# Down projection of a decoder layer: low parts of u in half tiles, adding transfers later, and one more pair by seven products

## The chip, the cores and the metric

The kernel runs on one core of one Trainium2 chip. The metric is the time of one execution on the device in microseconds (us), lower is better. The kernel before has a median of 1049.46 us over 3 runs (1048.84 to 1049.66).

## The reference, cut to what matters

One decoder layer on 256 positions of width 2048, in float32: a normed input projection, two attentions of 8 heads each, an output projection with a residual, and then an MLP with hidden width 8192. The change lies in the MLP:

```python
h = _rmsnorm(x, norm_mlp_pre[layer])
u = jnp.square(jax.nn.relu(h @ w_up[layer]))          # 256 x 8192
x = x + _rmsnorm(u @ w_down[layer], norm_mlp_post[layer])   # 8192 -> 2048
```

## The kernel before, in words

**Three matmuls for one product.** Every float32 operand is split into a high part (`hi`, ScalarE, line 306) and the remainder (`lo`, VectorE, line 307). A product is then hi·hi + lo·hi + hi·lo, that is three matmuls of 128x128 by 128x512. Weights come as `raw` tiles of 128x1024 (512 KB) on SyncE's queue and are split before use; a `Weights` object emits loads and splits up to six tiles ahead of TensorE.

**The down projection.** It runs in two halves of 1024 output columns (c = 0, 1), each over 64 blocks of 128 rows of u, which are taken as 32 pairs, numbered 0 to 31. A plain pair takes 2 x 4 products (24 matmuls). A pair in `DOWN_SEVEN[c]` is done by seven products of sums, after Strassen (21 matmuls). In the first half these are pairs 5, 7, 9, 11, then 15, 17, 19, 21, then 25, 27, 29; in the second every odd pair from 3 to 27. For such a pair p, GpSimd's queue fetches both weight blocks in one transfer of 1 MB (line 374, into `ab_down`, or by turns into `c` in the first half and `u01` in the second). VectorE makes the sums t and u of the weights (lines 361, 365, 366, destination `st_down`) and, for the u side, `four_sums` (lines 992 to 994) and their split into `s`. The sums of pair p are placed on VectorE ahead of the two `raw` splits of the plain pair p-1. In the first half the split `s` of a pair that both halves share is written to DRAM (`keep_s`); the second half reads it back (line 404) and needs neither `four_sums` nor the split.

**Where u's low part comes from.** u is produced in 16 tiles of four blocks (two pairs) each. While the up projection runs, `lo_away` writes -hi of a tile to DRAM (ScalarE, lines 960 and 962) and later adds u to it there (GpSimd's queue with an accumulating transfer, line 967), which leaves u - hi = lo in `ukeep`. In the down projection `split_u` makes `uhi` again on ScalarE and reads the whole low tile (512 KB) back into one of two `ulo` buffers on GpSimd's queue (line 979). Tile 0 is the exception: both times it is split on VectorE.

**What sets the order.** Each engine and each queue works in the order in which the program emits. GpSimd's queue is one such order: a transfer that waits there holds up all behind it. `Flow` is a clock by which chains such as `lo_away` are placed between matmuls; a `yield 16.0` puts the next step at least 16 us of that clock later.

**Between the halves.** The first half's four accumulators y are joined with the parts in `c` (line 1193), squared on ScalarE (line 1145) and multiplied by the gain (line 1197) in `half_evac`, while the second half begins.

Of the kernel before, what the change touches and what calls it, by code (L numbers as in the profile page):

```python
# [18 lines left out]
F32 = mybir.dt.float32  # L19
# [7 lines left out]
P = 128  # L27
# [236 lines left out]
def layer(nc, tc, io):  # L264
# [38 lines left out]
    def split(hi, lo, src, g=None):  # L303
        if g is not None:
            return split_gain(hi, lo, src, g)
        nc.scalar.activation(hi, src, AF.Copy)  # L306
        nc.vector.tensor_tensor(out=lo, in0=src, in1=hi.bitcast(F32), op=OP.subtract)  # L307
# [6 lines left out]
    def tok(t, k, b):  # L314
        return t[:, k, b * P:(b + 1) * P]
# [617 lines left out]
    def up_evac(j, b, i, acc, order):  # L933

        yield UP_STEP * order
        r = late["up"].tile([P, 512], F32, tag="r", bufs=2, name=f"r{j}_{b}")
        nc.scalar.activation(r, acc, AF.Relu, scale=rstd2[b])
# [12 lines left out]
        if b and j:  # L950
            flow.start(lo_away(j), 2.0 + 4.0 * (j % 2))

    def lo_away(g):

        ukeep[g] = dram.tile([P, CW], F32, name=f"ukeep{g}")
        u = uT[g].rearrange("p k s -> p (k s)")
        for h in range(2):
            c = slice(h * 512, (h + 1) * 512)
            t = late["up"].tile([P, 512], F32, tag="r", bufs=2, name=f"neg{g}_{h}")
            nc.scalar.activation(t.bitcast(F32R), u[:, c], AF.Copy, scale=-1.0)  # L960
            yield 1.0
            nc.scalar.dma_start(out=ukeep[g][:, c], in_=t)
            yield 7.0
        yield 16.0
        for h in range(2):
            c = slice(h * 512, (h + 1) * 512)
            nc.gpsimd.dma_start(out=ukeep[g][:, c], in_=u[:, c], accum_op=OP.add)
            yield 2.0

    def split_u(c, g):  # L970
        if (c, g) == (0, 0):
            uh, ul = [wp.tile([P, CW], F32R, tag=w, bufs=W_BUFS, name=f"u{w}0").rearrange("p (k s) -> p k s", k=4)
                      for w in ("hi", "lo")]
        else:
            uh, ul = [dpl["dp"].tile([P, 4, S], F32R, tag=f"u{w}", bufs=2, name=f"u{w}{c}_{g}") for w in ("hi", "lo")]
        u, h, l = [x.rearrange("p k s -> p (k s)") for x in (uT[g], uh, ul)]
        if g:
            nc.scalar.activation(h, u, AF.Copy)
            nc.gpsimd.dma_start(out=l.bitcast(F32), in_=ukeep[g])
# [153 lines left out]
    ssd = [con.tile([P, 4], F32, name=f"ssd{b}") for b in range(NB)]  # L1133

    def down_mm(c, u, k, b, n, w, first, last):
        three(y[b][2 * c + n], [tok(u[x], k % 4, b) for x in range(2)], [t[:, 0, n * 512:n * 512 + 512] for t in w],
              first, last)

    def spare(i, n):
# [3 lines left out]
    def square(n, b):  # L1143
        junk = dpl["dp"].tile([P, 512], BF16, tag="junk", bufs=1, name=f"junkd{n}{b}")
        nc.scalar.activation(junk, y[b][n], AF.Square, accum_out=ssd[b][:, n:n + 1])
# [41 lines left out]

    def half_evac(more, g_half):

        for n in range(2):  # L1190
            for b in range(NB):
                tt, out = nc.vector.tensor_tensor, more[b, n]
                tt(out=y[b][n], in0=y[b][n], in1=out, op=OP.add)
                yield 1.0
                square(n, b)
                yg[n, b] = out
                tt(out=out, in0=y[b][n], in1=g_half[n], op=OP.mult)
# [14 lines left out]
    for c in range(2):  # L1212

        for i, (b, n) in enumerate(PARTS):
            y[b][2 * c + n] = bank(4 * c + i, f"y{b}{2 * c + n}")
        accs = {(b, n): y[b][2 * c + n] for b, n in PARTS}
        ws = DOWN_SEVEN[c]
        for t, (what, k, tiles) in enumerate(wide_d[c]):
            g = (2 * k if what == "w" else k) // 4
            u = us[c, g]  # L1220
            if g >= GT - 2 and c:
                break
            if what == "k":
                w = weights.get(tiles[0])
                for b, n in PARTS:
                    down_mm(c, u, k, b, n, w, t == 0, t == len(wide_d[c]) - 1)
                    flow.pump()
                weights.free(tiles[0])
            else:
                if k == ws[0]:  # L1230
                    if not c:
                        flow.finish(*u_last)
                    else:
                        flow.finish(h_evac)
                    m = {i: bank(4 * (1 - c) + o, f"md{i}_{c}") for o, i in enumerate((1, 6, 7, 5))}
                blocks = [[tok(u[x], 2 * (k % 2) + kk, bb) for x in range(2)] for kk, bb in ((0, 0), (1, 0), (1, 1))]
                seven_products(tiles, (blocks, left.pop((c, k))), accs, m, k == ws[0], k == ws[-1])
                if k == ws[-1]:
                    more = close([spare(10, i) for i in range(4)] if c else closing(), m)
                if not c and k in SHARED:  # L1240
                    keep_s(k)
            nxt = (c, g + 1) if g < GT - 1 else (1, 0)
            if nxt not in us:
                us[nxt] = split_u(*nxt)
            if (c, what, k) == (0, "k", 3):
                weights.limit += 1
            if (c, what, k) == (0, "k", 36):
                g_half = [late["up"].tile([P, 512], F32, tag="r", bufs=2, name=f"g_half{n}") for n in range(2)]
                for n in range(2):
                    load_gain(n, g_half[n])  # L1250
            if (c, what, k) == (1, "k", 40):
                flow.start(x_back())
                for n in (2, 3):
                    load_gain(n, spare(4, n))
        if not c:
            h_evac = flow.start(half_evac(more, g_half))

    tail = {k: tiles[0] for what, k, tiles in wide_d[1] if k >= 4 * (GT - 2) and what == "k"}
    for g in (GT - 2, GT - 1):
        for b, n in PARTS:  # L1260
            for kk in range(4):
                k = 4 * g + kk
                w = weights.get(tail[k])
                if g < GT - 1:
                    down_mm(1, us[1, g], k, b, n, w, False, kk == 3)
                else:
                    three_more(y[b][2 + n], [tok(us[1, g][x], kk, b) for x in range(2)],
                               [t[:, 0, n * 512:n * 512 + 512] for t in w])
# [52 lines left out]
```

## Time and profile before

| what | value |
|---|---|
| median of 3 runs | 1049.46 us |
| the profiled execution | 1049.74 us |
| its span, first to last instruction | 1047.9 us |
| around the span | 1.8 us |
| granted TensorE clock, mean | 0.998 |
| TensorE busy | 1035.3 us (99%) |
| VectorE busy | 834.0 us (80%) |
| ScalarE busy | 644.5 us (62%) |
| DMA, mean over the span | 237 GB/s |

Times in the traces count from the span's start. The first half of the down projection runs from about 703 to 871.6 us, the second to about 1039 us; the up projection lies ahead of it from about 363 us on. A row of a timeline gives the start, the duration, the engine, the source line, the operation and its tiles (output, then inputs), how many instructions were merged, and in brackets how long the engine had been idle and what released it. For a DMA the duration is that of issuing it; "to landing" is from issue until its data has arrived.

### The profile page before, as it was taken

To read this page: it belongs to the slowest core of one execution; us is meant where nothing else is said; L and a number is where in the kernel's file an instruction comes from. 1 tells how busy PE (TensorE), PEld (TensorE's weight loads), DVE (VectorE), ACT (ScalarE), POOL (GpSimd) and SP (SyncE) were. 2 spreads that over 40 slices of the span, in tenths; PEclk is the share of its full clock that TensorE was granted. 3 is DMA by queue.
4 is the path that set the end of the run, shared out by engine and by line. 5 is a ranking of instruction groups with operands and counts; after the bars stand their busy time and mean duration, and the time that the engine had idled before them with its cause. 6 is when DMAs were issued, how large, how long until landed. Compare 5 with 4: busy or idle time off the path is not lost.

```text
span 1047.9 us, 13455 instructions
## 1 busy us (share of the span) xinstructions
PE 1035.3 (99%) x4828; PEld 860.3 (82%) x4828; DVE 834.0 (80%) x1122; ACT 644.5 (62%) x884; POOL 90.4 (9%) x134
## 2 busy tenths in 40 slices
PE   9999999999999999999999999999999999999996
PEld 6888889888888788888888888788888888788785
DVE  6676536567557669999999999796989888998895
ACT  6674436565555566675766767666757564866661
POOL 0000000000000000111101011011201001212100
PEclk9999999999999999999999999999999999999999
DMA  9975447454447295758879587589997977789862
GB/s 301 368 230 150 139 131 240 142 162 156 145 164 235 84 370 180 252 177 263 238 237 289 174 251 232 164 289 346 306 380 250 362 260 236 276 314 338 330 233 81
DMA packets 89395, 248.21 MB, mean 237 GB/s; under 512 B 7920, under 2 KB 12528, under 8 KB 88944
## 3 DMA queue, kind: packets, MB, share of 16 engines
q1 hardware_dynamic: 61984, 162.03, 45.9%
q0 software_dynamic: 22592, 77.08, 23.3%
q10 hardware_dynamic: 4752, 8.24, 2.2%
q8 instruction: 38, 0.62, 0.2%
q14 instruction: 29, 0.24, 0.1%
HBM read 222.16 MB, written 25.17 MB: 236 GB/s over the span
## 4 chain that ended last, share of the span: by engine, by line
PE 86%; DVE 6%; DMA 3%; issue 2%; ACT 2%; SPq 0%; POOL 0%; DVEq 0%; POOLq 0%; ACTq 0%
PE acc_u L296 21%; PE y L296 20%; PE acc_o L296 8%; PE m L296 6%; PE md L296 5%; PE acc_v L296 4%; PE acc_qk L296 4%; DVE lo L307 3%; PE acc_ckv L296 2%; PE acc_ukv L296 2%; PE acc_q L296 2%; PE acc_cq L296 2%; PE acc_k L296 2%; PE acc_uq L296 2%; PE rt L300 1%
## 5 line engine op out<-in xcount | busy, mean ns | idle before, releaser
L307 DVE TENSOR_TENSOR lo<-raw,hi 128x1024 fp32r<-128x1024 f32 (+3 forms) x207 | 233.5, 1149 | 81.8 <-ACT hi L306 81.1
L306 ACT ACTIVATE hi<-raw 128x1024 fp32r<-128x1024 f32 (+3 forms) x207 | 203.3, 996 | 67.4 <-DMA raw<-in_w_in 15.4
L296 PE MATMUL acc_u<-hi,hT_hi 128*128 128x512 f32 x356 | 141.7, 398 | 0.0
L296 PE MATMUL acc_u<-hi,hT_lo 128*128 128x512 f32 x356 | 139.2, 391 | 0.4 <-DVE hT_lo L307 0.4
L296 PE MATMUL acc_u<-lo,hT_hi 128*128 128x512 f32 x356 | 138.8, 390 | 0.0
L296 PE MATMUL y<-hi,ulo 128*128 128x512 f32 x352 | 137.1, 390 | 0.8 <-DMA ulo<-ukeep 0.8
L296 PE MATMUL y<-lo,uhi 128*128 128x512 f32 x352 | 137.1, 390 | 0.7 <-DVE lo L307 0.7
L296 PE MATMUL y<-hi,uhi 128*128 128x512 f32 x352 | 137.3, 390 | 0.0
L310 ACT ACTIVATE hi<-raw,gcol 128x1024 fp32r<-128x1024 f32 x74 | 83.0, 1147 | 31.9 <-DMA raw<-in_w_up 20.1
L311 DVE SCALAR_TENSOR_TENSOR lo<-raw,gcol,hi 128x1024 fp32r<-128x1024 f32 x74 | 92.4, 1278 | 11.1 <-ACT hi L310 11.0
L296 PEld LDWEIGHTS acc_u<-hi,hT_lo 128*128 128x128 f32 x356 | 66.8, 188 | 14.9 <-DVE hT_lo L307 0.8
L296 PEld LDWEIGHTS y<-hi,ulo 128*128 128x128 f32 x352 | 66.0, 188 | 15.0 <-DMA ulo<-ukeep 1.2
L296 PEld LDWEIGHTS y<-lo,uhi 128*128 128x128 f32 x352 | 66.1, 188 | 14.6 <-DVE lo L307 1.2
L296 PEld LDWEIGHTS acc_u<-lo,hT_hi 128*128 128x128 f32 x356 | 67.0, 188 | 13.0
L296 PEld LDWEIGHTS acc_u<-hi,hT_hi 128*128 128x128 f32 x356 | 66.9, 188 | 12.8
L296 PEld LDWEIGHTS y<-hi,uhi 128*128 128x128 f32 x352 | 66.1, 188 | 13.7
L306 ACT ACTIVATE hi<-u 128x1024 fp32r<-128x1024 f32 (+1 forms) x38 | 37.5, 990 | 47.6 <-DVE u L366 34.7
L307 DVE TENSOR_TENSOR lo<-st_down,hi 128x1024 fp32r<-128x1024 f32 x48 | 57.5, 1219 | 1.1 <-ACT hi L306 1.0
L296 PE MATMUL md<-hi,s 128*128 128x512 f32 x144 | 52.1, 389 | 0.0
L306 ACT ACTIVATE hi<-st_down 128x1024 fp32r<-128x1024 f32 x48 | 49.8, 1050 | 3.4 <-DVE st_down L366 2.9
L296 PE MATMUL acc_o<-hi,mixT_hi 128*128 128x512 f32 x128 | 51.8, 405 | 0.0
L296 PE MATMUL acc_o<-hi,mixT_lo 128*128 128x512 f32 x128 | 50.2, 392 | 0.0
(330 smaller groups left out, 2171.1 us busy)
## 6 DMA issues: line engine op xcount, KB each, us to landing
raw<-in_w_down SPq DMA_DIRECT2D x80, 512.0 KB, 6.1
raw<-in_w_up SPq DMA_DIRECT2D x76, 512.0 KB, 6.4
raw<-in_w_in SPq DMA_DIRECT2D x55, 512.0 KB, 5.1
ab<-in_w_up POOLq DMA_DIRECT2D x22, 1024.0 KB, 6.1
raw<-in_w_out SPq DMA_DIRECT2D x32, 512.0 KB, 4.4
ulo<-ukeep POOLq DMA_DIRECT2D x30, 512.0 KB, 6.7
ab_down<-in_w_down POOLq DMA_DIRECT2D x13, 1024.0 KB, 9.2
ukeep<-neg ACTq DMA_DIRECT2D x30, 256.0 KB, 4.4
```

The source lines that it names most:

```text
L296: nc.tensor.matmul(out, a, b, start=start, stop=stop)
L300: nc.tensor.transpose(out, a, ident)
L306: nc.scalar.activation(hi, src, AF.Copy)
L307: nc.vector.tensor_tensor(out=lo, in0=src, in1=hi.bitcast(F32), op=OP.subtract)
L310: nc.scalar.activation(hi, src, AF.Copy, scale=g)
L311: nc.vector.scalar_tensor_tensor(out=lo, in0=src, scalar=g, in1=hi.bitcast(F32), op0=OP.mult, op1=OP.subtract)
```

## The change

It does five things.

1. In the first half 12 pairs are done by seven products in place of 11: 5 to 15 and 19 to 29 by twos.
2. u's low tile is read back as two half tiles of 256 KB, one for each pair, into four buffers. `load_lo` numbers them by pair (0 to 31 in the first half, 32 to 63 in the second) and after the step of pair k emits the load for pair k+3.
3. Tile 0 goes through DRAM like the others, so that the second half reads its low part too and VectorE splits it once.
4. The adding transfers of `lo_away` come 34 us of the program's clock later in place of 16.
5. In `half_evac` the product by the gain of one accumulator comes behind the addition of the next.

How the instructions move on GpSimd's queue at the start of the down projection. The number behind `ulo0_` is the tile of two pairs, the number behind `ulo` in the new kernel is the pair; `ukeep` from `ab` are adding transfers of tiles 12 and 13; `ab_down` and `c` from `in_w_down` are the fetches for pairs 5, 7 and 9 in this order. Before:

```order
L979 DMA ulo0_1_6408<-ukeep1_3831 128x1024
L967 DMA ukeep12_6087<-ab_3502 128x512
L374 DMA ab_down_6373<-in_w_down 128x2x1024
L967 DMA ukeep12_6087<-ab_3502 128x512
L967 DMA ukeep13_6161<-ab_3502 128x512 x2
L979 DMA ulo0_2_6529<-ukeep2_4169 128x1024
L374 DMA c_3504<-in_w_down 128x2x1024
L979 DMA ulo0_3_6616<-ukeep3_4236 128x1024
L374 DMA ab_down_6373<-in_w_down 128x2x1024
```

And in the changed kernel:

```order
L989 DMA ulo2_6416<-ukeep1_3835 128x512
L989 DMA ulo3_6418<-ukeep1_3835 128x512
L374 DMA ab_down_6382<-in_w_down 128x2x1024
L989 DMA ulo4_6485<-ukeep2_4174 128x512
L989 DMA ulo5_6537<-ukeep2_4174 128x512
L989 DMA ulo6_6580<-ukeep3_4241 128x512
L967 DMA ukeep12_6093<-ab_3502 128x512
L374 DMA c_3504<-in_w_down 128x2x1024
L967 DMA ukeep12_6093<-ab_3502 128x512
L989 DMA ulo7_6628<-ukeep3_4241 128x512
L967 DMA ukeep13_6166<-ab_3502 128x512 x2
L989 DMA ulo8_6704<-ukeep4_4559 128x512
```

Before, the fetch for pair 7 (`c`) stands behind two low tiles, whose buffers are both empty. Now it stands behind `ulo6`, the fifth half tile, which needs the buffer of `ulo2` and so the end of pair 2. The next row behind the last shown is the fetch for pair 9, now behind `ulo8` and so behind the end of pair 4; before it stood behind `ulo0_3`, which needs the buffer of tile 1 and so the end of pair 3.

GpSimd's queue in the second half, around the fetch for pair 21 (the `u01` row). `s1_19` is the split that was kept for pair 19. Before:

```order
L374 DMA ab_down_6373<-in_w_down 128x2x1024
L404 DMA s1_19_8501<-skeep19_7299 128x1024
L979 DMA ulo1_9_8522<-ukeep9_5391 128x1024
L374 DMA u01_3505<-in_w_down 128x2x1024
L404 DMA s1_21_8584<-skeep21_7396 128x1024
```

In the changed kernel (half tile 52 belongs to pair 20 of the second half and needs the buffer of pair 16):

```order
L374 DMA ab_down_6382<-in_w_down 128x2x1024
L404 DMA s1_19_8573<-skeep19_7334 128x1024
L989 DMA ulo51_8593<-ukeep9_5396 128x512
L989 DMA ulo52_8652<-ukeep10_5712 128x512
L374 DMA u01_3505<-in_w_down 128x2x1024
L404 DMA s1_21_8658<-skeep21_7425 128x1024
```

Before, the fetch follows `s1_19`, which needs the end of pair 15. Now `ulo52` stands ahead of it, and the fetch follows the end of pair 16. The low part of pair 20, which stood behind the fetch and `s1_21` before, now stands ahead of both.

VectorE at the beginning of the second half. `y` are the first half's accumulators, `c` the parts joined to them. Before:

```order
L307 TENSOR_TENSOR lo_7825<-ab_down,hi_7824 128x512
L1193 TENSOR_TENSOR y_6374<-y_6374,c 128x512
L1197 TENSOR_TENSOR c<-y_6374,g_half_7240 128x512
L307 TENSOR_TENSOR lo_7849<-ab_down,hi_7848 128x1024
L1193 TENSOR_TENSOR y_6376<-y_6376,c 128x512
L1197 TENSOR_TENSOR c<-y_6376,g_half_7240 128x512
L307 TENSOR_TENSOR lo_7869<-st_down,hi_7868 128x1024
```

Changed:

```order
L307 TENSOR_TENSOR lo_7881<-ab_down,hi_7880 128x512
L1208 TENSOR_TENSOR y_6383<-y_6383,c 128x512
L1208 TENSOR_TENSOR y_6385<-y_6385,c 128x512
L307 TENSOR_TENSOR lo_7907<-ab_down,hi_7906 128x1024
L1203 TENSOR_TENSOR c<-y_6383,g_half_7269 128x512
L1208 TENSOR_TENSOR y_6384<-y_6384,c 128x512
L307 TENSOR_TENSOR lo_7927<-st_down,hi_7926 128x1024
```

The product by the gain (now line 1203) no longer stands right behind the addition to the same accumulator; another addition and a split lie between.

The diff:

```diff
-DOWN_SEVEN = ((5, 7, 9, 11, 15, 17, 19, 21, 25, 27, 29), range(3, 28, 2))
+DOWN_SEVEN = ((5, 7, 9, 11, 13, 15, 19, 21, 23, 25, 27, 29), range(3, 28, 2))
...
-        if b and j:
+        if b:
             flow.start(lo_away(j), 2.0 + 4.0 * (j % 2))
...
             nc.scalar.dma_start(out=ukeep[g][:, c], in_=t)
             yield 7.0
-        yield 16.0
+        yield 34.0
         for h in range(2):
...
     def split_u(c, g):
         if (c, g) == (0, 0):
-            uh, ul = [wp.tile([P, CW], F32R, tag=w, bufs=W_BUFS, name=f"u{w}0").rearrange("p (k s) -> p k s", k=4)
-                      for w in ("hi", "lo")]
-        else:
-            uh, ul = [dpl["dp"].tile([P, 4, S], F32R, tag=f"u{w}", bufs=2, name=f"u{w}{c}_{g}") for w in ("hi", "lo")]
-        u, h, l = [x.rearrange("p k s -> p (k s)") for x in (uT[g], uh, ul)]
-        if g:
-            nc.scalar.activation(h, u, AF.Copy)
-            nc.gpsimd.dma_start(out=l.bitcast(F32), in_=ukeep[g])
-        else:
-            split(h, l, u)
-        return uh, ul
+            uh, ul = [wp.tile([P, CW], F32R, tag=w, bufs=W_BUFS, name=f"u{w}0") for w in ("hi", "lo")]
+            split(uh, ul, uT[0].rearrange("p k s -> p (k s)"))
+            uh, ul = [x.rearrange("p (k s) -> p k s", k=4) for x in (uh, ul)]
+            return uh, [ul[:, 0:2], ul[:, 2:4]]
+        uh = dpl["dp"].tile([P, 4, S], F32R, tag="uhi", bufs=2, name=f"uhi{c}_{g}")
+        nc.scalar.activation(uh.rearrange("p k s -> p (k s)"), uT[g].rearrange("p k s -> p (k s)"), AF.Copy)
+        load_lo(2 * (c * GT + g) + 1)
+        return uh, [u_lo.pop(2 * (c * GT + g) + h) for h in range(2)]
+
+    u_lo = {}
+    next_lo = [2]
+
+    def load_lo(upto):
+
+        for i in range(next_lo[0], min(upto + 1, 4 * GT)):
+            g, h = i // 2 % GT, i % 2
+            t = u_lo[i] = dpl["dp"].tile([P, 2, S], F32R, tag="ulo", bufs=4, name=f"ulo{i}")
+            nc.gpsimd.dma_start(out=t.rearrange("p k s -> p (k s)").bitcast(F32), in_=ukeep[g][:, h * 512:(h + 1) * 512])
+            next_lo[0] = i + 1
...
     def half_evac(more, g_half):
 
+        def half_gain(b, n):
+            yg[n, b] = more[b, n]
+            nc.vector.tensor_tensor(out=more[b, n], in0=y[b][n], in1=g_half[n], op=OP.mult)
+
+        done = []
         for n in range(2):
             for b in range(NB):
-                tt, out = nc.vector.tensor_tensor, more[b, n]
-                tt(out=y[b][n], in0=y[b][n], in1=out, op=OP.add)
+                nc.vector.tensor_tensor(out=y[b][n], in0=y[b][n], in1=more[b, n], op=OP.add)
+                square(n, b)
                 yield 1.0
-                square(n, b)
-                yg[n, b] = out
-                tt(out=out, in0=y[b][n], in1=g_half[n], op=OP.mult)
-                yield 1.0
+                if done:
+                    half_gain(*done.pop())
+                    yield 1.0
+                done.append((b, n))
+        half_gain(*done.pop())
...
+            load_lo(2 * c * GT + (k if what == "w" else k // 2) + 3)
             nxt = (c, g + 1) if g < GT - 1 else (1, 0)
             if nxt not in us:
                 us[nxt] = split_u(*nxt)
```

More of the change, by code (lines that the diff above doesn't have):

```diff
@@ L971, in split_u, with utok @@
         if (c, g) == (0, 0):
-            uh, ul = [wp.tile([P, CW], F32R, tag=w, bufs=W_BUFS, name=f"u{w}0").rearrange("p (k s) -> p k s", k=4)
-                      for w in ("hi", "lo")]
-        else:
-            uh, ul = [dpl["dp"].tile([P, 4, S], F32R, tag=f"u{w}", bufs=2, name=f"u{w}{c}_{g}") for w in ("hi", "lo")]
-        u, h, l = [x.rearrange("p k s -> p (k s)") for x in (uT[g], uh, ul)]
-        if g:
-            nc.scalar.activation(h, u, AF.Copy)
-            nc.gpsimd.dma_start(out=l.bitcast(F32), in_=ukeep[g])
-        else:
-            split(h, l, u)
-        return uh, ul
+            uh, ul = [wp.tile([P, CW], F32R, tag=w, bufs=W_BUFS, name=f"u{w}0") for w in ("hi", "lo")]
[14 more added lines that the diff above has]
+            next_lo[0] = i + 1
+    def utok(u, x, k, b):
+        return tok(u[1][k // 2], k % 2, b) if x else tok(u[0], k, b)
     def keep_s(kp):
@@ L1135, in down_mm @@
     def down_mm(c, u, k, b, n, w, first, last):
-        three(y[b][2 * c + n], [tok(u[x], k % 4, b) for x in range(2)], [t[:, 0, n * 512:n * 512 + 512] for t in w],
+        three(y[b][2 * c + n], [utok(u, x, k % 4, b) for x in range(2)], [t[:, 0, n * 512:n * 512 + 512] for t in w],
               first, last)
@@ L1235, in layer @@
                     m = {i: bank(4 * (1 - c) + o, f"md{i}_{c}") for o, i in enumerate((1, 6, 7, 5))}
-                blocks = [[tok(u[x], 2 * (k % 2) + kk, bb) for x in range(2)] for kk, bb in ((0, 0), (1, 0), (1, 1))]
+                blocks = [[utok(u, x, 2 * (k % 2) + kk, bb) for x in range(2)] for kk, bb in ((0, 0), (1, 0), (1, 1))]
                 seven_products(tiles, (blocks, left.pop((c, k))), accs, m, k == ws[0], k == ws[-1])
@@ L1266, in layer @@
                 else:
-                    three_more(y[b][2 + n], [tok(us[1, g][x], kk, b) for x in range(2)],
+                    three_more(y[b][2 + n], [utok(us[1, g], x, kk, b) for x in range(2)],
                                [t[:, 0, n * 512:n * 512 + 512] for t in w])
```

## The prediction

> **What bounds the kernel now.** I read the page first, then TensorE's waits, then the timeline around two of them, then who was late there.
>
> ```profile
> PE 1035.3 (99%) x4828; PEld 860.3 (82%) x4828; DVE 834.0 (80%) x1122; ACT 644.5 (62%) x884; POOL 90.4 (9%) x134
> ```
>
> All waits of TensorE (us in total, times, longest), and a row of the chain that ended last (start, us, what):
>
> ```profile
> PE warm L521 <- DVE zero L518: 1.2, 1, 1.2
> PE y L296 <- DMA ulo<-ukeep: 0.8, 1, 0.8
> PE y L296 <- DVE lo L307: 0.7, 1, 0.7
> PE rt L300 <- ACT r L937: 0.7, 1, 0.7
> PE acc_u L296 <- DVE hT_lo L307: 0.4, 1, 0.4
> PE qrt L300 <- DVE qT L772: 0.2, 1, 0.2
> ```
>
> ```profile
> 987.02 5.44 PE y L296 x24
> ```
>
> TensorE is the bound: in the down projection (tiles `y`) it waits twice. A matmul takes 5.44 / 24 = 0.2267 us when nothing holds it, so a plain pair takes 5.44 us and a pair by seven products 21 x 0.2267 = 4.76 us. A gain can come only from fewer matmuls or from these two waits; anything else matters only if it makes a new one. The timeline of TensorE at the two places:
>
> ```profile
> 892.91 0.39 PE L296 MATMUL y<-hi,uhi 128*128 128x512 f32 x1
> 894.04 0.50 PE L296 MATMUL y<-lo,uhi 128*128 128x512 f32 x1 [0.74 <-DVE lo L307]
> 894.37 0.40 PE L296 MATMUL y<-hi,ulo 128*128 128x512 f32 x1
> ...
> 975.79 0.39 PE L296 MATMUL y<-lo,uhi 128*128 128x512 f32 x1
> 976.98 0.50 PE L296 MATMUL y<-hi,ulo 128*128 128x512 f32 x1 [0.80 <-DMA ulo<-ukeep]
> 977.31 0.39 PE L296 MATMUL y<-hi,uhi 128*128 128x512 f32 x1
> ```
>
> The first costs 894.37 - 892.91 - 2 x 0.2267 = 1.01 us (bracket plus the slow restart), the second, worked out alike, 977.31 - 975.79 - 0.45 = 1.07 us.
>
> **The change part by part.** *The twelfth pair* takes 24 - 21 = 3 matmuls away: -0.68 us. What it adds lies on VectorE, below.
>
> *Closing work, and tile 0 through DRAM.* VectorE before the first wait: a timeline row, and its waits between 876 and 890.5 us (total, times, longest):
>
> ```profile
> 868.06 1.22 DVE L307 TENSOR_TENSOR ulo<-u,uhi 128x1024 fp32r<-128x1024 f32 x1
> ...
> 892.77 2.35 DVE L307 TENSOR_TENSOR lo<-raw,hi 128x1024 fp32r<-128x1024 f32 x2
> ```
>
> ```profile
> DVE c L1197 <- ACT junkd L1145: 3.2, 4, 0.8
> DVE lo L307 <- ACT hi L306: 1.7, 3, 1.2
> ```
>
> TensorE waited at 894.04 for the first of the two splits at 892.77. Ahead of it VectorE idled 3.2 us behind ScalarE's squares and 1.7 us behind its high parts, and split tile 0 for 1.22 us. The new order puts work between an addition and its product by the gain, so most of the 3.2 us go, and the 1.22 us go whole: over 4 us against a need of 1.01. What is late next is pair 5's fetch; its sums may start as late as 3.8 us (worked out below) before TensorE's 893.1, that is at 889.3. By the order it follows a half tile that needs pair 0's buffer, free at 871.6 + 5.44 = 877.0; issued at 878 and with the 9.6 us seen below it lands at 887.7. So -1.0 us. The extra -hi writes and adds of tile 0 fall about 400 to 440 us, where tile 1's lie already and none of the six waits does: 0.
>
> *Low parts in half tiles.* The load that TensorE waited for at 976.98 stood on GpSimd's queue behind the kept split. It was the only one issued between 960 and 970 us:
>
> ```profile
> DMA to landing us min/median/max: 10.6/10.6/10.6
> ```
>
> It had the 10.2 us of two pairs. Now pair 20's half is asked for when pair 16 ends, three pairs (about 15 us) ahead of use, and stands ahead of the fetch. So -1.07 us. Sum of the gains: -0.68 - 1.01 - 1.07 = -2.76 us.
>
> *What the half tiles put in front of the fetches* is the price. GpSimd's timeline:
>
> ```profile
> 707.67 2.08 POOL L374 DMA_DIRECT2D c<-in_w_down  x1
> 727.45 0.55 POOL L979 DMA_DIRECT2D ulo<-ukeep  x1 [17.70 <-PE y L296]
> 728.00 0.70 POOL L374 DMA_DIRECT2D ab_down<-in_w_down  x1
> ...
> 738.66 0.70 POOL L374 DMA_DIRECT2D c<-in_w_down  x1 [1.82 <-DVE lo L307]
> ```
>
> These are the fetches for pairs 7, 9 and 11. By the order shown above, fetch p now stands behind a half tile that waits for pair p-5's end; before, it stood behind one that waits for pair p-6. That is one pair, about 5.4 us, later. How long a fetch may take then comes from VectorE and TensorE at pair 6:
>
> ```profile
> 731.68 1.23 DVE L361 TENSOR_TENSOR st_down<-c 128x1024 f32<-128x1024 f32 x1 [2.10 <-DMA c<-in_w_down]
> ...
> 734.28 2.35 DVE L307 TENSOR_TENSOR lo<-raw,hi 128x1024 fp32r<-128x1024 f32 x2
> ...
> 742.32 1.23 DVE L361 TENSOR_TENSOR st_down<-ab_down 128x1024 f32<-128x1024 f32 x1
> ...
> 752.95 1.22 DVE L361 TENSOR_TENSOR st_down<-c 128x1024 f32<-128x1024 f32 x1
> ```
>
> ```profile
> 737.19 0.39 PE L296 MATMUL y<-hi,uhi 128*128 128x512 f32 x1
> 737.41 0.39 PE L296 MATMUL y<-lo,uhi 128*128 128x512 f32 x1
> ```
>
> The sums start at 731.68, pair 6's first low part is done 3.8 us after that (734.28 + 1.22 = 735.50), TensorE reads it at 737.41: 1.9 us to spare. VectorE then needs 752.95 - 742.32 = 10.63 us for a plain pair and a seven, TensorE 5.44 + 4.76 = 10.20. So each further plain pair of a run of sevens has 0.43 us less. Runs were of four; now they are of six, and the last of them loses 4 x 0.43 = 1.72 us of the 1.9. A run of six just fits, with 0.2 us over, if no sums start late.
>
> Pair 6 starts at 737.19, so pair 4 ends at 737.19 - 4.76 = 732.43, and pair 2 at 732.43 - 2 x 5.44 = 721.55. The row at 727.45 shows 0.46 us from a pair's end (pair 3: 726.99) to the issue, and the fetch follows 0.55 us later, or 1.1 with an add between. Fetch 7 is thus issued at about 723.1 (was 707.67) and has to land by 731.4: 8.3 us. Fetch 9 is issued at 733.4 (was 728.00) and its sums may start 0.2 later than 742.32, so it has to land by 742.1: 8.6 us. How long they take, over the first half (`ab_down`, then `c`), and for the two issued at 728.00 and 738.66:
>
> ```profile
> DMA to landing us min/median/max: 8.8/9.6/14.3
> ...
> DMA to landing us min/median/max: 7.8/12.8/23.6
> ...
> DMA to landing us min/median/max: 11.4/11.4/11.4
> ...
> DMA to landing us min/median/max: 8.2/8.2/8.2
> ```
>
> These shared the queue with 512 KB of a low tile ahead of them; now it is 256 KB, but four adding transfers of 256 KB of tiles 12 and 13, which "later" moves from about 704 to about 723 to 729 us, stand between fetches 7 and 9. I take 10.1 us for fetch 9, between 8.2 and 11.4: VectorE starts 1.5 us late, and since the run has no reserve TensorE waits 1.5 us in all in pairs 8 to 14. The ends are 0 (8.2) and 4.5 us (fetch 7 at the median of 12.8).
>
> [...] The view of `ukeep` from 746.9 to 749 us:
>
> ```profile
> L967 POOL DMA_DIRECT2D ukeep<-uT x4: 924/1422/1921, 747.0 to 748.7; - x4
> ...
> DMA to landing us min/median/max: 7.0/9.9/11.4
> ```
>
> Five loads are in it, a low tile first (7.0) and then the adds, 0.57 us apart. The median, 9.9, is the second add's: landed at 757.5; the last at 748.7 + 11.4 = 760.1. [...]
>
> *Second run (19 to 29).* Fetch 19 keeps its old place; fetch 21 waits for pair 16. From there to pair 20's first low part are 2 x 5.44 + 4.76 + 0.22 = 15.86 us; less 1.0 to issue, 0.4 from landing to the sums, 3.8 to the low part and 1.72 for the run leaves 8.9 us. Against a median of 9.6 with twice as much low tile ahead I take 9.3: +0.4. Ends 0 and +3.9 (12.8).
>
> *Second half.* There VectorE needs less per pair (shared pairs skip `four_sums` and the split), so the limit is 5.44 + 2 x 4.76 + 0.22 - 5.2 = 10.0 us with no run term. Only x, read back about 960 us, presses on it. The DMA view from 955 to 970 us (KB each, median us to landing):
>
> ```profile
> uT<-xkeep SPq DMA_DIRECT2D x4, 512.0 KB, 10.1
> ...
> u<-in_w_down POOLq DMA_DIRECT2D x1, 1024.0 KB, 9.7
> ...
> ab_down<-in_w_down POOLq DMA_DIRECT2D x1, 1024.0 KB, 15.0
> ```
>
> Fetch 21 moves from 956.7 into this crowd. I take 10.4, nearer to its own 9.7 than to the 15.0 of the next one, which had 1 MB ahead of it: +0.4; ends 0 and +5.
>
> **Sum.** -2.76 + 1.5 + 0.4 + 0.4 = -0.46 us on the profiled 1049.74, which is 0.28 above the median. From the median: 1049.0 us. A difference under 0.2% (2.1 us) cannot be told from no change here.
>
> **The rivals.** *All fetches land in time* (under 8.6 us): the whole -2.76, 1046.7 us. For it: half the low tile ahead of each, and 8.2 and 8.8 have been seen. Against: medians of 9.6 and 12.8.
>
> *The fetches become the bound* (slower). One mechanism: in a run of six VectorE has no reserve, and every microsecond that a fetch takes beyond 8.3 to 8.9 us is a microsecond of TensorE. At 11.4 us for fetch 9 (+2.8), 12 for fetch 21 (+3.1) and 12 in the second half (+2.0): 7.9 - 2.76 = +5.1, 1054.6 us. It decides the sign from 2.76 us of lateness on in all. For it: the first half's DMA engines are busy already, and two fetches there took over 12.
>
> *"Later" moves nothing in the up projection.* TensorE's wait of 0.7 us for `r` lies there, and GpSimd did this some 20 us before it:
>
> ```profile
> 648.15 0.74 POOL L374 DMA_DIRECT2D ab<-in_w_up  x1 [14.80 <-DVE lo L307]
> 648.89 3.61 POOL L967 DMA_DIRECT2D ukeep<-ab  x4
> ```
>
> The adds of tiles 10 and 11 stand right behind the same fetch in the new order, so they are issued at 648.9 again and the 0.7 us stay; my sum has it so. Were they to move, the time would be 0.7 us lower, 1048.3.
>
> **Chances.** The forecast (partly late fetches, within 2.1 us of the median, the third rival among it) 0.49; all or nearly all in time 0.29; fetches as the bound, over 2.1 us slower, 0.22. The range goes from 1046.6 (all gains) to 1052.8, about half way to the slow case. Its own range for the likeliest case is 1047.4 to 1051.5.
>
> **What would show it.** Right: both waits above gone; the fetch for pair 9 issued at about 733 us; new waits of TensorE for `lo` in pairs 8 to 14 of the first half, with VectorE waiting for `c` or `ab_down` at the head of its sums; 3 matmuls fewer. Wrong: VectorE's sums never late and no new wait (first rival), or waits for `lo` of several us in both runs (second). A wait for `ulo` anywhere would mean that the loads are too late even three pairs ahead.

## The result, and the profile after

The changed kernel takes 1058.32 us (median of 4 executions, 1057.09 to 1061.87), the kernel before beside it 1049.56 (4 executions): a ratio of 1.0089 with a 95% interval of 1.0064 to 1.0115. It is slower, by some 9 us; the forecast was 1049.0 us, within 1046.6 and 1052.8. The profiled execution is the longest of the four, 1061.87 us with a span of 1060.0, so 12.1 us over the profiled execution before.

The page's first line, and all waits of TensorE:

```profile
PE 1039.4 (98%) x4825; PEld 860.9 (81%) x4825; DVE 836.3 (79%) x1126; ACT 646.0 (61%) x888; POOL 111.7 (11%) x170
```

```profile
PE y L296 <- DVE lo L307: 5.8, 4, 2.3
PE md L296 <- ACT uhi L977: 1.6, 1, 1.6
PE rt L300 <- ACT r L937: 1.3, 1, 1.3
PE warm L521 <- DVE zero L518: 1.2, 1, 1.2
PE acc_qk L296 <- ACT hi L306: 0.8, 1, 0.8
PE acc_u L296 <- DVE hT_lo L307: 0.4, 1, 0.4
PE qrt L300 <- DVE qT L772: 0.2, 1, 0.2
```

The 3 matmuls are gone (4825, not 4828), the wait for `ulo` too, but four new ones for `lo` have come. The first stands at pair 8 of the first half. GpSimd's queue ahead of it, with the fetches for pairs 7 (`c`) and 9 (`ab_down`):

```profile
722.92 0.54 POOL L989 DMA_DIRECT2D ulo<-ukeep  x1 [15.46 <-PE y L296]
723.45 0.92 POOL L967 DMA_DIRECT2D ukeep<-ab  x1
724.02 1.07 POOL L374 DMA_DIRECT2D c<-in_w_down  x1
...
733.80 0.58 POOL L989 DMA_DIRECT2D ulo<-ukeep  x1 [3.08 <-PE md L296]
734.37 0.73 POOL L374 DMA_DIRECT2D ab_down<-in_w_down  x1
```

Fetch 9 stands behind the half tile that waited for pair 4's end, and is issued at 734.37 us (728.00 before). Its transfer, by the DMA view of that microsecond (KB, us to landing), and what VectorE and TensorE then do:

```profile
ab_down<-in_w_down POOLq DMA_DIRECT2D x1, 1024.0 KB, 12.7
```

```profile
743.70 1.22 DVE L307 TENSOR_TENSOR lo<-st_down,hi 128x1024 fp32r<-128x1024 f32 x1
747.17 1.23 DVE L361 TENSOR_TENSOR st_down<-ab_down 128x1024 f32<-128x1024 f32 x1 [2.25 <-DMA ab_down<-in_w_down]
748.43 0.69 DVE L365 TENSOR_TENSOR st_down<-st_down,ab_down 128x512 f32<-128x512 f32 x1
749.16 0.69 DVE L366 TENSOR_TENSOR st_down<-st_down,ab_down 128x512 f32<-128x512 f32 x1
749.77 2.35 DVE L307 TENSOR_TENSOR lo<-raw,hi 128x1024 fp32r<-128x1024 f32 x2
```

```profile
748.32 0.39 PE L296 MATMUL y<-hi,uhi 128*128 128x512 f32 x1
751.04 0.50 PE L296 MATMUL y<-lo,uhi 128*128 128x512 f32 x1 [2.34 <-DVE lo L307]
751.38 0.39 PE L296 MATMUL y<-hi,ulo 128*128 128x512 f32 x1
...
752.48 0.63 PE L296 MATMUL y<-hi,uhi 128*128 128x512 f32 x1
752.91 0.63 PE L296 MATMUL y<-lo,uhi 128*128 128x512 f32 x1
753.34 0.63 PE L296 MATMUL y<-hi,ulo 128*128 128x512 f32 x1
```

The data land at 734.37 + 12.7 = 747.1, VectorE's queue stands on the sums, and behind them, three operations later, is the split that TensorE needs for pair 8, whose own `raw` tile was there by 743.57 us, when ScalarE began its high part. Two things are to be seen on TensorE: a pause of 751.04 - 748.32 - 0.23 = 2.5 us, and, 1 us after its end, eight matmuls 0.427 us apart (752.91 - 752.48) in place of 0.227: 8 x 0.2 = 1.6 us more, in which nothing is waited for. The granted TensorE clock in the trace is 0.50 there (752.1 to 755.4 us) and 1.00 from 760 to 765 us.

In the second half the same happens once more, behind the fetch for pair 23:

```profile
994.78 0.39 PE L296 MATMUL y<-hi,uhi 128*128 128x512 f32 x1
997.26 0.50 PE L296 MATMUL y<-lo,uhi 128*128 128x512 f32 x1 [2.09 <-DVE lo L307]
```

And in the second run of the first half TensorE waits a little in every plain pair, first behind fetch 21, then to the run's end at 858 us (five times; the first and the last):

```profile
814.46 0.39 PE L296 MATMUL y<-hi,uhi 128*128 128x512 f32 x1
815.16 0.50 PE L296 MATMUL y<-lo,uhi 128*128 128x512 f32 x1 [0.31 <-DVE lo L307]
...
857.18 0.39 PE L296 MATMUL y<-hi,uhi 128*128 128x512 f32 x1
857.70 0.50 PE L296 MATMUL y<-lo,uhi 128*128 128x512 f32 x1
```

The 12.1 us, worked out from the distances between TensorE's matmuls (over 0.227 us) at each place of both traces:

| place | us |
|---|---|
| first run, behind fetch 9: pause 2.61, half speed 1.58 | +4.19 |
| second run, behind fetch 21: 0.58, then four times 0.40 | +2.19 |
| closing work, 896.8 and 901.7 us: 1.87 and 1.28 | +3.15 |
| second half, behind fetch 23: pause 2.37, half speed 1.58 | +3.95 |
| wait for `r` in the up projection (1.50, was 0.81), and the kernel's first microseconds (0.25) | +0.9 |
| behind the last matmul 0.2, and 0.3 that is not placed | +0.5 |
| what the forecast counted as gains, gone from this trace: 0.68, 1.01, 1.07 | -2.76 |
| sum | +12.1 |

### The profile page after: what moved, and what is told of

It is laid out like the page before. It is cut to its first block, busy times and chain, and to the rows that moved or that the text cites. A ratio compares the mean times of both kernels' runs of the same rounds, so it can differ in the third digit from the quotient of the medians.

```text
span 1060.0 us, 13520 instructions
## 1 busy us (share of the span) xinstructions
PE 1039.4 (98%) x4825; PEld 860.9 (81%) x4825; DVE 836.3 (79%) x1126; ACT 646.0 (61%) x888; POOL 111.7 (11%) x170
## 4 chain that ended last, share of the span: by engine, by line
PE 74%; DVE 9%; DMA 7%; issue 6%; ACT 2%; POOL 1%; SPq 0%; DVEq 0%; POOLq 0%; ACTq 0%
PE acc_u L296 21%; PE y L296 11%; PE acc_o L296 8%; PE m L296 6%; DVE lo L307 4%; PE acc_v L296 4%; PE acc_qk L296 4%; DMA ab_down<-in_w_down 3%; PE md L296 3%; PE acc_ckv L296 2%; PE acc_ukv L296 2%; PE acc_q L296 2%; PE acc_cq L296 2%; PE acc_k L296 2%; PE acc_uq L296 2%
## 5 line engine op out<-in xcount | busy, mean ns | idle before, releaser
L307 DVE TENSOR_TENSOR lo<-raw,hi 128x1024 fp32r<-128x1024 f32 (+3 forms) x205 | 231.1, 1148 | 80.0 <-ACT hi L306 78.4
L296 PEld LDWEIGHTS acc_u<-hi,hT_hi 128*128 128x128 f32 x356 | 66.9, 188 | 12.7
L989 POOL DMA_DIRECT2D ulo<-ukeep x62 | 34.3, 554 | 269.7 <-PE md L296 134.9
L307 DVE TENSOR_TENSOR lo<-st_down,hi 128x1024 fp32r<-128x1024 f32 x50 | 59.9, 1218 | 3.5 <-ACT hi L306 3.5
L296 PE MATMUL md<-hi,s 128*128 128x512 f32 x150 | 54.4, 390 | 1.6 <-ACT uhi L977 1.6
```

The costliest lines, as they stand in the source:

```text
L296: nc.tensor.matmul(out, a, b, start=start, stop=stop)
L989: nc.gpsimd.dma_start(out=t.rearrange("p k s -> p (k s)").bitcast(F32), in_=ukeep[g][:, h * 512:(h + 1) * 512])
```

## The experiments

The theories are named in the expectations: Q, the place of the fetch on GpSimd's queue; V, VectorE's load from the twelfth pair; A, the adding transfers; C, the order of the closing work. Ratios are against the kernel before, run in turn with each on the same chip.

### The place of the fetch: e1, e15, e5

The half tile for pair k+3 is emitted after pair k. With k+2 (and `down_mm` taking it from `u_lo` when it is used) fetch p stands behind the half tile that waits for pair p-6, with k+4 behind the one for p-4.

```diff
-            load_lo(2 * c * GT + (k if what == "w" else k // 2) + 3)
+            load_lo(2 * c * GT + (k if what == "w" else k // 2) + 2)
```

Expected of e1:

> The changed kernel, but each half tile of low parts is asked for one pair later in program order, so that the fetch of pair p stands on GpSimd's queue behind the half tile that waits for pair p-6's end, as it did before the change, and no longer behind the one for p-5. Nothing else is changed. If the place of the fetch is the cause (theory Q), fetch 9 is issued about 5 us earlier (near 729 us, not 734.4), the wait of 2.5 us at 748 us, the one of 2.25 us at 995 us and the chain of 0.3 to 0.5 us waits between 814 and 858 us go, and the time falls by 8 to 11 us to about 1048 to 1050 us. If VectorE's load from the twelfth pair is the cause (theory V), the chain between 814 and 858 us and the closing waits near 897 and 902 us stay, and it gives 1053 to 1055. If the adding transfers on the same queue are the cause (theory A), the wait at 748 us stays nearly whole: 1055 to 1058.

Measured: 1047.86 us, ratio 0.998 (0.9971 to 0.999). Again beside e13 and e16:

> The kernel of the first experiment again, beside e13 and e16 on the same chip: 1047.9 us, 0.2% faster than the kernel before, with an interval that leaves out 1.

Measured: 1048.92 us, ratio 0.9991 (0.9982 to 1.0). That interval reaches 1, against what was expected. The two together put this kernel some 0.15% below the kernel before, which the intervals barely tell from nothing. What is clear is that this edit alone makes it about 10 us faster than the changed kernel. TensorE's largest waits in e1, and GpSimd's queue and the DMA view at fetch 9:

```profile
PE rt L300 <- ACT r L937: 1.4, 1, 1.4
PE warm L521 <- DVE zero L518: 1.2, 1, 1.2
PE acc_u L296 <- DVE hT_lo L307: 0.4, 1, 0.4
```

```profile
728.17 0.57 POOL L990 DMA_DIRECT2D ulo<-ukeep  x1 [3.08 <-PE y L296]
728.73 0.73 POOL L374 DMA_DIRECT2D ab_down<-in_w_down  x1
```

```profile
ab_down<-in_w_down POOLq DMA_DIRECT2D x1, 1024.0 KB, 12.4
```

No wait for `lo`, `ulo` or `uhi` is left (in e15's trace one for `lo`, of 0.5 us at 893 us). Fetch 9 took as long as in the changed kernel (12.4 against 12.7 us); it was issued 5.6 us earlier, and so nobody waited. The twelve pairs, with no reserve on VectorE, do no harm then, so theory V falls.

The other way, as a dose, e5 (k+4):

> The other way from the first experiment: the changed kernel, but each half tile is asked for one pair earlier still, so that the fetch of pair p stands behind the half tile that waits for pair p-4's end. The work is the same, only this place moves. Theory Q (the fetch's place sets the time): after pair p-4's end there are 10.2 us until TensorE needs the split behind the fetch's sums (two pairs), against some 13 us that the chain takes (issue, 8 to 9 us of transfer, 2.6 us of sums, 1.2 us of split), so TensorE waits about 3 us at each of the 25 pairs by seven products, and after such a wait it may run 3.4 us at half clock (1.6 us each): 1120 to 1170 us. If VectorE's load or the adding transfers are the cause (theories V and A), the place adds nothing: 1058 to 1062 us.

Measured: 1093.06 us, ratio 1.0407 (1.0373 to 1.044). TensorE's waits:

```profile
PE y L296 <- DVE lo L307: 26.0, 13, 6.3
PE md L296 <- ACT uhi L977: 3.5, 1, 3.5
PE y L296 <- ACT uhi L977: 2.9, 1, 2.9
```

The three places give 1047.9, 1058.3 and 1093.1 us for the same work: theory Q holds. The size was guessed too high: TensorE waits for `lo` in 13 places, not in all 25. That its pauses let VectorE catch up is a likely reason, but no run tests it.

### The other edits undone on the changed kernel: e2, e3, e4

e2, the eleven pairs:

```diff
-DOWN_SEVEN = ((5, 7, 9, 11, 13, 15, 19, 21, 23, 25, 27, 29), range(3, 28, 2))
+DOWN_SEVEN = ((5, 7, 9, 11, 15, 17, 19, 21, 25, 27, 29), range(3, 28, 2))
```

> The changed kernel with the eleven pairs of before in the down projection's first half; the other edits stay. The twelfth pair's 3 matmuls come back: +0.68 us. Theory V (VectorE has no reserve in runs of six): the chain of waits between 814 and 858 us (2.2 us) and the closing waits (3.1 us) go, the wait at 748 us gets smaller as VectorE has a plain pair more to catch up: 1052 to 1054 us. Theory Q (the fetches' place): the waits at 748 and 995 us stay (2.6 and 2.4 us, and 1.6 us each where TensorE's clock falls after them), so no lower than 1055 us.

Measured: 1064.15 us, ratio 1.0137 (1.0116 to 1.0159), a miss for every theory: 6 us slower than with twelve pairs. GpSimd's queue and VectorE at the fetch for pair 17 (here and below the expectations miscount it as that of pair 15):

```profile
779.07 0.57 POOL L989 DMA_DIRECT2D ulo<-ukeep  x1 [4.47 <-PE y L296]
779.63 0.89 POOL L967 DMA_DIRECT2D ukeep<-uT  x1
780.18 1.08 POOL L374 DMA_DIRECT2D c<-in_w_down  x1
```

```profile
782.78 1.22 DVE L307 TENSOR_TENSOR lo<-st_down,hi 128x1024 fp32r<-128x1024 f32 x1
796.02 1.22 DVE L361 TENSOR_TENSOR st_down<-c 128x1024 f32<-128x1024 f32 x1 [12.02 <-DMA c<-in_w_down]
```

With this list a fetch comes directly behind the later adds of tiles 14 and 15, lands 15.8 us after its issue, and TensorE pauses 5.4 us. With twelve pairs three plain pairs (16 to 18) lie there. So e2 cannot judge theory V (the chain between 814 and 858 us is indeed gone from its trace, but a worse wait has come ahead of it); e1 does. With the fetch in the changed kernel's place the later adds need the new list.

e3, `half_evac` with the body that the diff removes:

> The changed kernel with the closing work in the order of before (addition, square, product by the gain, for one piece after the other). Theory C (the interleaved order makes VectorE and ScalarE wait for each other in turn, 6.3 us on VectorE in place of 4.9): the waits near 897 and 902 us (1.9 and 1.3 us) shrink by the 1.4 us that VectorE gains, 1056 to 1057 us. If those waits come only from VectorE being late already when the closing work begins, no change: 1058. By the forecast's reading, in which the interleaved order saves over 3 us there, this run would be slower: 1060 to 1061.

Measured: 1058.79 us, ratio 1.0085 (1.007 to 1.01): no difference to the changed kernel's 1.0089. C falls, and so does the forecast's reading; what came out is the second case, VectorE late already when the closing work begins.

e4, `yield 34.0` back to `yield 16.0`:

> The changed kernel with the adding transfers started as early as before (16 units, not 34). Theory A (the later adds hold back fetches 7 and 9 and slow their transfers to 12.7 us): the wait at 748 us goes, with the half-clock stretch behind it, and with it part of the chain at 814 us: 1053 to 1055 us. Theory Q: fetch 9 still waits for pair 4's end near 733 us behind its half tile, and the earlier adds crowd the fetches at the start of the down projection as before: 1057 to 1059 us.

Measured: 1056.14 us, ratio 1.006 (1.0045 to 1.0075). The wait at pair 8 went, two smaller ones came at pairs 12 and 14 (1.1 and 0.3 us), the others stayed, the one in the second half shorter (1.6 us, no half speed). The adds are a smaller part, of 2 us, on top of the place. At fetch 9 they are the whole of it:

```profile
734.16 0.71 POOL L374 DMA_DIRECT2D ab_down<-in_w_down  x1
```

```profile
ab_down<-in_w_down POOLq DMA_DIRECT2D x1, 1024.0 KB, 8.5
```

It is issued as late as in the changed kernel (734.37) and stands behind the same half tile, but without the adds it lands after 8.5 us in place of 12.7, and TensorE does not wait at pair 8. At this fetch the late place and the slow transfer are both needed for the wait: e1 takes away the one, e4 the other.

### With the fetch in its old place: e6, e7, e8, e12, e16

Each is e1 with one more edit undone; e16 has the old closing work and `yield 25.0`.

> The kernel of the first experiment (half tile behind the fetch, 1047.9 us) with the closing work in the order of before. What the interleaved order is worth when no fetch is late: by the forecast it saves VectorE over 3 us and takes away 1.0 us of TensorE's time near 893 us, together with tile 0 through DRAM, so without it the wait for lo near 893 us comes back in part: 1048.3 to 1048.9 us. If the interleaving saves nothing (VectorE idled 6.3 us in it against 4.9 us before) and the wait went because of tile 0 or the half tiles: 1047.4 to 1047.9 us.

> The kernel of the first experiment with the eleven pairs of before. If the twelfth pair is worth what its 3 matmuls take and VectorE keeps up with it, this is 0.68 us slower than 1047.9: 1048.5 us. If VectorE's missing reserve in the longer runs costs something, it is faster: 1047.0 to 1047.8. If the list of pairs and the time of the adding transfers only fit together (with eleven pairs the adds of tiles 14 and 15 stand directly ahead of the fetch of pair 15, which landed 15.8 us after its issue in the second experiment), a wait near 790 us stays and it gives 1050 to 1053 us.

> The kernel of the first experiment with the adding transfers as early as before (16 units). If the later start is worth nothing by itself: 1047.6 to 1048.2 us. If the adds of tiles 12 to 15, now beside the first fetches of the down projection again, make fetches of pairs 5 to 9 land later (23.6 us after its issue for pair 7 in the kernel before) and the twelve pairs leave no reserve for that: 1049 to 1052 us. The wait of 1.4 us for the transposes at 668 us, 0.7 us before the change: if the later adds make it, it goes back to 0.7 and the time falls by that.

> The kernel of the first experiment (1047.9 us) with tile 0's low part in the down projection's second half made by VectorE again (two halves of 0.6 us each) and not kept in DRAM. If that 1.2 us is what took the wait near 893 us away, it comes back in part: 1048.3 to 1048.9 us. If the kernel has enough reserve there once the low parts come in half tiles: 1047.9. If tile 0's added transfers are what made the wait for the transposes at 668 us grow from 0.7 to 1.4 us, it goes back: 1047.2 us.

> The kernel of the first experiment with the closing work as before and the adding transfers started at 25 units, between 16 and 34. At 16 units it was 1050.1 us, at 34 units 1047.9 (closing work either way). If the gain comes from keeping the adds away from the first fetches: between these, 1048 to 1050. If 34 already crowds later fetches (that of pair 15 took 11.3 us): under 1047.9.

| kernel | us | ratio | interval |
|---|---|---|---|
| e1 | 1047.86 | 0.998 | 0.9971 to 0.999 |
| e6, closing work as before | 1048.07 | 0.9981 | 0.9971 to 0.999 |
| e7, eleven pairs | 1050.06 | 0.9999 | 0.9989 to 1.0009 |
| e8, adds at 16 | 1050.15 | 0.9993 | 0.9984 to 1.0003 |
| e12, tile 0 on VectorE | 1051.25 | 1.0011 | 1.0001 to 1.0021 |
| e16, closing as before, adds at 25 | 1051.18 | 1.0015 | 1.0006 to 1.0024 |

The interleaved closing work gives nothing. With it, tile 0 through DRAM is needed: without it `md` waits 2.1 us for `uhi` at 890 us (e12, with a stretch at half speed behind it). The old closing work with tile 0 on VectorE was not run in this place. e7 is 0.19% (2.0 us) slower than e1: 0.68 us of it are the twelfth pair's matmuls, and 1.4 us are waits for `lo` between 790 and 812 us, behind a fetch for pair 17 that took 17.6 us beside the later adds. A start of the adds between the two values is worse than either; e16's trace shows waits from 738 us on, behind a fetch for pair 7 that took 18.5 us.

### One edit alone on the kernel before: e9, e14, e10, e11, e13

> The kernel before with the interleaved closing work and nothing else of the change. The forecast gives this edit, with tile 0, the whole wait for lo near 893 us: 1.0 us faster, 1049.2 us against 1050.2 in the last runs of the kernel before. If the interleaved order only moves VectorE's waiting from ScalarE's squares to ScalarE's high parts (6.3 us idle in the changed kernel against 4.9 us before): no gain, 1050.0 to 1051 us, and the wait of 0.7 us at 893 us stays or grows.

Measured: 1051.42 us, ratio 1.0011 (1.0001 to 1.0021). The profiled execution of the ten took 2128 us, for a reason that stays open; it is not in the ratio, and its trace is not used. e14 is the same kernel again:

> The kernel of the ninth experiment again, for its trace: the kernel before with only the interleaved closing work. If the interleaving makes VectorE and ScalarE wait for each other, VectorE idles over 5 us for ScalarE's high parts between 876 and 892 us (4.9 us in all before, 3.2 of it for the squares), and TensorE's wait for lo near 893 us is 0.7 us or more. By the forecast's reading VectorE idles under 2 us there and TensorE does not wait.

Its one execution took 1049.81 us. VectorE's waits between 868 and 893 us, the kernel before had 3.2 us for `junkd` and 1.7 us for `hi` there:

```profile
DVE lo L307 <- ACT hi L306: 6.3, 3, 2.8
```

The same in the changed kernel, VectorE first and then ScalarE:

```profile
890.22 0.69 DVE L1208 TENSOR_TENSOR y<-y,c 128x512 f32<-128x512 f32 x1
892.67 1.22 DVE L307 TENSOR_TENSOR lo<-st_down,hi 128x1024 fp32r<-128x1024 f32 x1 [1.76 <-ACT hi L306]
```

```profile
891.01 0.60 ACT L1156 ACTIVATE junkd<-y 128x512 bf16<-128x512 f32 x1 [2.56 <-DVE y L1208]
891.50 0.19 ACT L1156 ACTIVATION_READ_ACCUMULATOR junkd<-y 128x1 f32 x1
891.59 1.05 ACT L306 ACTIVATE hi<-st_down 128x1024 fp32r<-128x1024 f32 x1
```

The product no longer waits for the square. But the square waits for VectorE's addition, the high part stands behind the square on ScalarE, and the split that is next on VectorE waits for that high part: the wait has moved and grown by 1.4 us.

> The kernel before with the twelve pairs and nothing else of the change. The forecast: 3 matmuls less, 0.68 us faster, if the fetches land in time: 1049.5 us. If the twelve pairs need the later adding transfers, since the adds of tiles 14 and 15 (747 to 760 us) now stand beside the fetches of pairs 11 and 13: waits for lo between 760 and 860 us, 1050.5 to 1053 us.

Measured: 1051.72 us, ratio 1.0012 (1.0002 to 1.0023). Its trace has no new wait among the fetches; the wait for `lo` at 893 us grows from 1.0 to 1.9 us. That execution took 1049.25 us, so what makes the median 2.5 us longer is not in it.

> The kernel before with the later adding transfers and nothing else of the change. The forecast costs and credits this edit at next to nothing: 1050.2 us. If the later adds of tiles 14 and 15 now stand directly ahead of the fetch of pair 15, as in the second experiment, where that fetch landed 15.8 us after its issue: a wait for lo near 790 us and 1051 to 1055 us. The wait for the transposes at 668 us grows from 0.7 to 1.4 us if the later adds of tiles 8 and 9 (633 us) are its cause; it stayed 1.4 us with the early adds in the fourth and eighth experiment, which speaks against that.

Measured: 1054.13 us, ratio 1.0039 (1.0026 to 1.0052). As in e2, fetch 17 is right behind the adds and takes 18.1 us, TensorE pauses 2.4 us at 791 us and then runs at half speed. The wait for `r` was 1.4 us.

> The kernel before with only the half tiles (behind the fetch, as in the first experiment) and tile 0's low parts through DRAM: eleven pairs, early adding transfers, closing work as before. The forecast's terms for these two edits are 1.07 us (the wait for ulo at 976 us) and, with tile 0, up to 1.01 us (the wait for lo at 893 us): 1048.1 to 1049.1 us against 1050.2 for the kernel before. If the twelve pairs and the later adds carry the gain of the first experiment only as a pair: near 1048.5, so that the pair is worth 0.7 us. If the half tiles' more numerous transfers (64 in place of 30 and tile 0's) take back what they give: 1050.

Measured: 1049.49 us, ratio 0.9995 (0.9986 to 1.0005): the waits for `ulo` and `lo` are gone from its trace, but the wait for `r` is 1.4 us, with one more of 0.3 us before it, so little is left of the 2.08 us. (e13 holds two edits; neither was run alone.) None of these kernels is measurably faster than the one before. The later adds are slower alone, by 0.4%; the twelve pairs and the interleaved closing work by 0.1%, with intervals that only just leave out 1. With the fetches in their old place the ratios speak for twelve pairs and later adds together: 0.998, 0.9981 and 0.9991 with both (e1, e6, e15), 0.9999 and 0.9993 with one of them (e7, e8), 0.9995 with neither (e13). The intervals overlap, and e13 and e15, measured side by side, differ by 0.0004, so it is not shown.

## Why the prediction was wrong, point by point

**The mechanism was right.** Fetch p behind pair p-5's end, VectorE's queue standing on the sums, no reserve in a run of six, and waits for `lo` at plain pairs: the trace shows all of it, and fetch 9 was issued at 734.4, forecast at 733.4. In the second run the waits behind fetch 21, four times 0.40 us, are the 0.43 us by which the forecast had VectorE fall back at each plain pair.

**The limits were right, the durations were not.** This is the step that failed: "I take 10.1 us for fetch 9", "I take 9.3", "I take 10.4", from which the terms 1.5, 0.4 and 0.4 us of the sum come. All three were taken 2.1 to 2.6 us too short.

| fetch | limit forecast | taken | measured | over the limit | TensorE waited | half speed behind it |
|---|---|---|---|---|---|---|
| 9, first run | 8.6 | 10.1 | 12.72 | 4.1 | 2.61 | 1.58 |
| 21, second run | 8.9 | 9.3 | 11.39 | 2.5 | 2.19 | none |
| 23, second half | 10.0 | 10.4 | 12.49 | 2.5 | 2.37 | 1.58 |

The limits hold: in the last two rows TensorE waited about what the fetch took beyond its limit, and in e4, where fetch 9 took 8.53 us, it did not wait at pair 8. In the first row 2.61 and the 3 x 0.43 us that pairs 10, 12 and 14 should have waited make 3.9. Those three waits did not come: TensorE lost 1.58 us at half speed there, which is time that VectorE gained. That the whole loss, 4.19 us, is so near to 4.1 is thus luck. (Fetch 7 passed its limit too, with 9.86 us against 8.3; it made no wait of its own, since fetch 9 was later still.)

Each duration came from rows that were not the nearest. *Fetch 9:* the forecast named the four adds that move with it, and took 10.1 all the same; e4 shows them to be the difference between 8.5 and 12.7 us. *Fetch 21:* in the new list it is the second fetch of its run, and the second fetches of the three runs before (pairs 7, 17 and 27) took 23.6, 13.0 and 12.8 us. In the traces with eleven pairs it took 6.3 to 9.0 us, with twelve 10.5 to 12.0 (8.5 in e5); what slows it in that place was not isolated. *Second half:* the forecast priced fetch 21, which took 7.5 us. The late one was fetch 23, which had already taken 15.0 us before and stands a pair later like the rest, and which the sum put at nothing. It met the end of x's read-back (the last of its transfers, issued at 974.1 us, took 13.4 us) and 1 MB of `raw` (two transfers, 10.6 and 12.0 us). In e1 it took 14.5 us, but was issued early enough, and nobody waited.

**The rival that came true** is the second one, "the fetches become the bound": 1054.6 us at 11.4, 12 and 12 us. At the measured durations the sum is 4.1 + 2.5 + 2.5 - 2.76 = +6.3, 1056 us; the median was 1058.3. Three late fetches come from one cause and are not independent, so 0.22 was too little, and the range should have reached the slow case; its upper end, 1052.8, is two thirds of the way there from 1049.0, not half.

**The half speed was put at nothing:** 3.2 us in the profiled execution.

**The closing work** was to give 1.0 us. With the fetch in its old place the wait at 893 us is gone (e1, e6; one of 0.5 us in e15), but not by the reason given: interleaving is worth nothing (e6, e9), and with it tile 0 is needed (e12). "Most of the 3.2 us go" overlooked that the square keeps its place ahead of the high part on ScalarE. In the changed kernel 3.15 us were lost there, because VectorE came late into the second half. From the sums of pair 3 to the last two products by the gain it needs the same 19.05 us in both traces (878.96 to 898.01, in e1 868.70 to 887.75), but it begins 0.3 us after that half has begun (878.6) in place of 3.1 us ahead (871.8). Two things lie behind this. It was still behind from the second run: the split before those sums ends 0.8 us ahead of the half's start, in e1 3.7 us. And it then waited 1.16 us for fetch 3 (0.59 in e1), which moved from 21.0 to 11.2 us ahead of the half's start. The forecast began with pair 5's fetch and priced neither.

**The twelfth pair's 0.68** came out as matmuls: 4825, not 4828.

**The half tiles' 1.07** is not shown as a gain. No kernel with half tiles has a wait for `ulo` in its trace. But e10, e11 and e14 read whole low tiles in the second half, with these loads as they were before the change, and their traces have no such wait either. It stood in the one execution from which the forecast was made, and a median need not have it. e13, at 0.9995, fits that.

**The third rival** said that the wait for `r` stays at 0.7. It was 1.3 or 1.4 us in the changed kernel and in every kernel with half tiles; 1.4 with the later adds alone (e11), 1.2 with twelve pairs alone (e10), whose code up to there is that of before, 0.5 in e14. Part of it changes between executions; which edit makes the rest stays open.

**Also open:** why the changed kernel's median lies 3.5 us under its profiled execution. The mean clock granted was 0.995 there and 0.998 in the three others; 0.003 x 1060 = 3.2 us is what the two half-speed stretches cost, so they may have been missing there. Those executions have no trace. Of e8's 2 us over e1 its trace shows pauses of 0.5, 0.4 and 0.3 us (664, 780 and 894 us); the rest is not placed.

## What to carry to other kernels

Before a load is put ahead of another on an in-order queue, see what it waits for: the transfer behind it inherits that wait. Here fetch 9 was issued 0.55 us behind a low tile of 512 KB for which the queue had waited 17.70 us in the kernel before, and 0.57 us behind a half tile of 256 KB for which it had waited 3.08 us in the changed one. When a transfer is moved, take its duration from the crowd that it moves into, and when several stand on one limit, let the range reach the case in which all are late. Look for a wait in more than one execution before it is counted as a gain. Test an edit that is meant to shorten a wait between two engines in the order of both: it may only move the wait to the other's queue.

## What the runs showed of the hardware

After some of its pauses TensorE ran at half speed for a while, without any wait. In the traces of all these kernels (e9's aside) none of the 31 pauses of 1.0 to 1.8 us in the stream of matmuls was followed by it. Of 16 of 2.0 to 6.5 us, 14 were; two in e5, of 2.25 and 3.05 us, were not, while another of 2.25 us, in the changed kernel, was. After the 11 of them up to 3.7 us the matmuls are 0.427 us apart for about 3.4 us (8 x 0.427), beginning 0.2 to 1.4 us after the pause: 1.6 us more. In the three longer pauses (4.6, 5.4 and 6.5 us) the granted clock fell to 0.5 before the pause was over and stayed there for 6.8 us, which cost 1.7 to 2.7 us behind it. So the pause of 2.5 us at pair 8 cost 4.1. The granted clock, as the mean of the profiled execution, was 0.995 in the changed kernel, 0.992 in e2, 0.994 in e3, 0.987 in e5, 0.996 in e11 and 0.995 in e12, and 0.997 or 0.998 in all others but e9. What decides whether the half speed follows a pause is not shown.
